# Nine raw weight buffers in the room of a smaller DMA scratch

## The chip, the cores and the metric

The kernel runs on one core of a Trainium2 chip. The core has a matrix engine (PE, with its weight loads told apart as PEld), a vector engine (DVE), a scalar engine (ACT), a general engine (POOL) and a queue engine that only issues and waits (SP). Each runs its own instructions in order. DMA transfers are issued by SP, ACT or POOL and run beside the engines. The metric is the time of one execution on the device in microseconds; lower is better.

## The reference

One layer (DEPTH is 1) of a streaming encoder with 256 frames of 2048 channels, all in float32. Cut to what matters:

```python
mod = silu(c) @ w_ada + b_ada                    # 6 vectors of 2048
sh1, sc1, g1, sh2, sc2, g2 = split(mod, 6)
h = rmsnorm(x, norm_g[0]) * (1 + sc1) + sh1
y = token_mixer(h, ...)                          # h @ w_in (2048 x 10256), linear attention with a
                                                 # forget gate, a gated short convolution, merge, @ w_o
x = x + g1 * rmsnorm(y, norm_g[1])
h = rmsnorm(x, norm_g[2]) * (1 + sc2) + sh2
gate, up = split(h @ w_up, 2)                    # 2048 x 11264
y = (gelu(causal_dwconv(gate)) * up) @ w_down    # 5632 x 2048
x = x + g2 * rmsnorm(y, norm_g[3])
```

`c` is a single vector, so `silu(c) @ w_ada` is a product of a vector with a matrix of 2048 x 12288. The weights are read once each.

## The kernel before

**Tiles and chunks.** All weights pass through the core as a *stream* of pieces, in the order in which they are used. A piece is loaded into a raw buffer, prepared, and used. There are three kinds:

- `Chunk`: 256 rows by 512 columns of a weight (128 partitions x 1024 floats, 512 KB). `dma` loads it (L278). `split` writes a rounded copy on ACT (`whi`, L283) and the rest on DVE (`wlo = raw - whi`, L292). `mm` multiplies it on PE, as three products: high by high, high by low and low by high. Groups of the kind `Feat` (L346) keep the weight still, groups of the kind `Tok` (L401) the activations.
- `Gemv`: 128 rows by 1024 columns of `w_ada` (512 KB, L431). It has no matmul: DVE adds `raw * silu(c)[k]` to a running sum (L439).
- `Ada`: the same for the first two vectors, which `h` needs (loads at L465, updates at L479), by slices of the channels.

When a sum of gemvs is complete, `fold` (L204 to L212) transposes it into a raw buffer (L209) and reduces it (L211).

**Raw buffers.** All of these take their buffer from one pool of `RAW_BUFS` tiles of 4 KB of a partition, under the tag `raw`. A buffer comes free when its last reader is done, which for a chunk is the split on DVE.

**What sets the order.** `pump` (L510) goes through the stream. For each piece it first issues loads ahead, then splits ahead, then multiplies:

```python
while pos[0] < min(len(stream), i + 1 + look_dma) and pos[0] < pos[1] + RAW_BUFS:
    stream[pos[0]].dma()
    pos[0] += 1
while pos[1] < min(len(stream), i + 1 + LOOK_SPLIT, ...):
    ...
```

`pos[0]`, `pos[1]` and `pos[2]` count the pieces loaded, split and multiplied. Splits run up to four pieces ahead of the matmuls (`LOOK_SPLIT`), loads up to ten (`LOOK_DMA`), which is also four and the six raw buffers. The framework's planner then lays out each engine's queue by its own costs, the priorities and the buffers that it takes to be free; it may place an instruction earlier than the text has it.

**The stages.** First come the pieces of `Ada` for the first slice of channels, the norm of `x` and the start of `h`. Then the input projection runs in five slices of the channels, with the gemvs merged in between the chunks (L918 to L933). It is followed by the rest of the token mixer, `late` (L935 to L959): the output of the convolution, the gates, the linear attention's heads beside them as small steps (`gla_heads`, L746: per head two groups of small matmuls, L758 and L772, a square on ACT, L776, a sum on DVE, L779, and a matmul with ones, L782), its output and `w_o`. `to_rows` (L816) sends the vectors g1 and g2 through DRAM and back to all partitions, with DMAs that POOL issues (L824, L827); these rows are read at L841 and L1027. Between the halves stands a norm (from L1128, with `x` loaded again at L1116). Then the channel mixer runs in three parts of `w_up` and `w_down`.

[...]

Of the kernel before, what the change touches and what calls it, by code (L numbers as in the profile page):

```python
# [34 lines left out]
C_CB, C_CC, C_CX = 3088, 4112, 5136  # L35
C_GA, C_GB = 6160, 8208

RAW_BUFS, SPLIT_BUFS, LOOK_SPLIT, LOOK_DMA = 6, 4, 4, 10
T1 = 4
T2 = 4  # L40
G8 = 4
# [1180 lines left out]
```

## Time and profile before

| | us |
|---|---|
| median of 3 runs | 1451.01 |
| lowest, highest | 1450.29, 1453.19 |
| the profiled execution | 1448.84 |
| its span, from first to last instruction | 1447.1 |
| mean granted clock of PE | 0.993 |

The profile tells of one execution. A row of a group has the line, the engine, the operation, the tiles written and read, how many there were, the time they were busy, the mean of one in ns, and the idle time of the engine before them with what ended it. A row of the timeline has the start, the time it took, the engine, the line, the operation and its tiles; in brackets stands how long the engine was idle before it and who ended that. A row of the waits has who waited for whom, the sum in us, how often, and the longest. `SPq` is SP's queue, which issues the loads. Matmuls overlap, so the busy time of PE counts a matmul until its modelled end. An idle engine costs something only where the end of the kernel waits for it.

### The profile page before, as it was taken

The numbers are of one execution on the slowest core, as the hardware profiler recorded it, in microseconds if no ns is written. First come the engines' busy times: TensorE is split into PE (matmuls) and PEld (weight loads), VectorE is DVE, ScalarE is ACT, GpSimd is POOL, SyncE is SP. The second block draws the span as 40 slices with busy tenths as digits, with TensorE's granted clock in tenths as the row PEclk, the third lists the DMA queues.
The fourth block names the chain that finished last, engine by engine and source line by source line (L and its number), as shares of the span: only waits on it lengthen the run. The fifth ranks groups of instructions, "written<-read, shape, count | busy, mean of one in ns | idle before, by whom it ended". The sixth has DMA issues, their size and how long they took to land.

```text
span 1447.1 us, 23205 instructions
## 1 busy us (share of the span) xinstructions
PE 1407.4 (97%) x9107; PEld 1262.5 (87%) x9107; DVE 1058.6 (73%) x1194; ACT 816.9 (56%) x995; POOL 6.1 (0%) x40
## 2 busy tenths in 40 slices
PE   6999999999999998999999999999999999999997
PEld 6898999898999998988898888888888888888886
DVE  6878888888888777976798777556767645566565
ACT  5789776688574554444665554444545533445553
POOL 0000000000000000000000000000000000000000
PEclk9999999999999999999999999999999999999999
DMA  9999999998979777897467777777786656666652
GB/s 318 329 329 329 373 317 334 335 307 293 355 249 327 244 257 269 293 313 246 134 201 243 227 243 231 248 236 233 230 251 202 217 195 190 186 196 190 190 185 95
DMA packets 177896, 366.82 MB, mean 253 GB/s; under 512 B 13803, under 2 KB 26457, under 8 KB 177018
## 3 DMA queue, kind: packets, MB, share of 16 engines
q1 hardware_dynamic: 176857, 362.17, 76.0%
q0 software_dynamic: 352, 2.11, 0.4%
q8 instruction: 71, 1.16, 0.3%
q10 hardware_dynamic: 576, 1.05, 0.2%
q14 instruction: 40, 0.32, 0.1%
HBM read 363.18 MB, written 2.11 MB: 252 GB/s over the span
## 4 chain that ended last, share of the span: by engine, by line
PE 76%; DMA 11%; DVE 7%; ACT 3%; issue 2%; SPq 0%; DVEq 0%; ACTq 0%
PE mm L346 50%; PE mm L401 25%; DMA raw<-in_w_ada_dram 7%; DMA raw<-in_w_in_dram 4%; DVE wlo L292 2%; ACT whi L283 1%; DVE c L439 1%; DVE c L479 1%; DVE fold L211 0%; PE sm L1152 0%; ACT mm L323 0%; DVE raw L209 0%; PE sm L782 0%; ACT t L257 0%; DVE XF L1138 0%
## 5 line engine op out<-in xcount | busy, mean ns | idle before, releaser
L283 ACT CAST whi<-raw 128x1024 fp32r<-128x1024 f32 (+1 forms) x503 | 513.1, 1025 | 499.1 <-PE mm L346 202.9
L292 DVE TENSOR_TENSOR wlo<-raw,whi 128x1024 fp32r<-128x1024 f32 (+1 forms) x503 | 594.7, 1190 | 245.9 <-ACT whi L283 242.0
L346 PE MATMUL mm<-H,whi 128*128 128x256 f32 (+2 forms) x3712 | 656.9, 321 | 2.2 <-ACT H L254 1.2
L346 PEld LDWEIGHTS mm<-H,whi 128*128 128x128 f32 x3712 | 527.8, 189 | 51.5 <-ACT whi L283 1.7
L346 PE MATMUL mm<-H,wlo 128*128 128x256 f32 (+1 forms) x2496 | 365.9, 278 | 1.4 <-DVE wlo L292 1.4
L346 PEld LDWEIGHTS mm<-H,wlo 128*128 128x128 f32 x2496 | 332.6, 188 | 14.4 <-DVE wlo L292 1.6
L401 PE MATMUL mm<-whi,g 128*128 128x512 f32 x704 | 178.3, 391 | 0.0
L401 PEld LDWEIGHTS mm<-whi,g 128*128 128x128 f32 x704 | 131.9, 188 | 29.1
L439 DVE SCALAR_TENSOR_TENSOR c<-raw,sil,c 128x1024 f32<-128x1024 f32 x90 | 115.3, 1281 | 42.3 <-DMA raw<-in_w_ada_dram 42.1
L401 PE MATMUL mm<-whi,H 128*128 128x512 f32 x448 | 117.5, 394 | 4.2 <-ACT whi L283 4.2
L401 PEld LDWEIGHTS mm<-whi,H 128*128 128x128 f32 x448 | 82.9, 188 | 24.0 <-ACT whi L283 6.4
L401 PE MATMUL mm<-wlo,g 128*128 128x512 f32 x352 | 98.1, 392 | 0.0
L479 DVE SCALAR_TENSOR_TENSOR c<-raw,sil,c 128x768 f32<-128x768 f32 (+2 forms) x73 | 78.6, 1077 | 8.8 <-DMA raw<-in_w_ada_dram 8.1
L401 PEld LDWEIGHTS mm<-wlo,g 128*128 128x128 f32 x352 | 66.1, 188 | 14.1
L401 PE MATMUL mm<-wlo,H 128*128 128x512 f32 x224 | 65.3, 393 | 0.0
L439 DVE SCALAR_TENSOR_TENSOR cb<-raw,sil,cb 128x1024 f32<-128x1024 f32 x30 | 38.5, 1284 | 24.8 <-DMA raw<-in_w_ada_dram 24.8
L401 PEld LDWEIGHTS mm<-wlo,H 128*128 128x128 f32 x224 | 42.2, 188 | 9.0
L618 DVE SCALAR_TENSOR_TENSOR t<-pt,fcol,t 128x256 f32<-128x256 f32 x88 | 36.6, 481 | 0.0
L346 PE MATMUL mm<-B,whi 128*128 128x256 f32 x256 | 33.4, 283 | 0.0
L346 PEld LDWEIGHTS mm<-B,whi 128*128 128x128 f32 x256 | 30.8, 188 | 2.6 <-issue 1.2
L346 PE MATMUL mm<-g,whi 128*128 128x256 f32 x256 | 32.3, 279 | 0.0
L346 PEld LDWEIGHTS mm<-g,whi 128*128 128x128 f32 x256 | 30.8, 190 | 0.0
(196 smaller groups left out, 740.8 us busy)
## 6 DMA issues: line engine op xcount, KB each, us to landing
raw<-in_w_up_dram SPq DMA_DIRECT2D x176, 512.0 KB, 4.3
raw<-in_w_ada_dram SPq DMA_DIRECT2D x160, 512.0 KB, 5.5
raw<-in_w_in_dram SPq DMA_DIRECT2D x145, 512.0 KB, 5.5
raw<-in_w_down_dram SPq DMA_DIRECT2D x88, 512.0 KB, 4.3
raw<-in_w_o_dram SPq DMA_DIRECT2D x32, 512.0 KB, 5.5
raw<-in_w_ada_dram SPq DMA_DIRECT2D x32, 384.0 KB, 5.6
raw<-in_w_out_conv_dram SPq DMA_DIRECT2D x16, 512.0 KB, 5.3
raw<-in_w_out_gla_dram SPq DMA_DIRECT2D x16, 512.0 KB, 5.0
```

Source lines behind the costliest of these rows:

```text
L283: nc.scalar.copy(self.hi, self.raw)
L292: nc.vector.tensor_sub(self.lo, self.raw, f(self.hi))
L346: nc.tensor.matmul(out, w[:, t, j * P:(j + 1) * P], x, start=first_in_bank and t == 0 and i == 0, stop=end and t == ch.n - 1 and i == 2, s ...
L401: nc.tensor.matmul(self.out[s], m(c.k0 + t, T)[:, s * P:(s + 1) * P], w[:, t, :], start=first and t == 0 and i == 0, stop=end and t == c.n ...
L439: nc.vector.scalar_tensor_tensor(a, self.raw, sil[:, self.k:self.k + 1], a, op0=ALU.mult, op1=ALU.add)
L479: nc.vector.scalar_tensor_tensor(a, raw, sc, a, op0=ALU.mult, op1=ALU.add)
L618: nc.vector.scalar_tensor_tensor(dst[:, a, :], pt[:, a, i:T + i], w(i, a), dst[:, a, :], op0=ALU.mult, op1=ALU.add)
```

## The change

The scratch for dynamic DMAs is set to 4 KB of a partition. The raw pool has nine buffers instead of six, and loads are issued up to thirteen pieces ahead of the matmuls instead of ten. The other look-aheads and all instructions of the text stay as they are.

```diff
-RAW_BUFS, SPLIT_BUFS, LOOK_SPLIT, LOOK_DMA = 6, 4, 4, 10
+RAW_BUFS, SPLIT_BUFS, LOOK_SPLIT, LOOK_DMA = 9, 4, 4, 13
...
-    nc = _bacc.Bacc("TRN2", target_bir_lowering=False, num_devices=1)
+    nc = _bacc.Bacc("TRN2", target_bir_lowering=False, num_devices=1, dynamic_dma_scratch_size=4096)
```

## The prediction

> **What bounds the kernel now.** I read the page first (busy shares, the 40 slices, the chain by line, the landing times), then the windows view stage by stage, then the waits of PE and of SP.
>
> ```profile
> PE 1407.4 (97%) x9107; PEld 1262.5 (87%) x9107; DVE 1058.6 (73%) x1194; ACT 816.9 (56%) x995; POOL 6.1 (0%) x40
> DMA  9999999998979777897467777777786656666652
> PE 76%; DMA 11%; DVE 7%; ACT 3%; issue 2%; SPq 0%; DVEq 0%; ACTq 0%
> raw<-in_w_in_dram SPq DMA_DIRECT2D x145, 512.0 KB, 5.5
> ```
>
> The stages, from the windows view:
>
> ```profile
> 0.00:40.00 40.00, 27.15 (x199) 26.08 (x200) 25.90 (x43) 23.89 (x37) 1.39 (x12) 0.96 0.96 320
> 40.00:600.00 560.00, 544.06 (x4406) 519.38 (x4405) 465.62 (x495) 379.44 (x432) 1.59 (x6) 0.99 0.91 310
> 600.00:680.00 80.00, 80.00 (x382) 66.86 (x382) 61.60 (x57) 37.01 (x46) 0.00 (x0) 1.00 0.85 286
> 680.00:720.00 40.00, 36.89 (x226) 32.54 (x225) 27.59 (x49) 24.85 (x50) 0.00 (x0) 0.91 0.47 141
> 720.00:1440.00 720.00, 719.29 (x3902) 617.61 (x3900) 474.29 (x547) 351.36 (x430) 3.10 (x22) 1.00 0.66 209
> ```
>
> The columns of a window are: PE, PEld, DVE, ACT and POOL busy, the granted clock, the DMA share, GB/s. There are two regimes. From 720 us on PE is idle for 0.71 of 720 us while DMA runs at 0.66: earlier loads have nothing to end there. From 600 to 680 PE is never idle. From 680 to 720 PE loses 3.1 us in the norm between the halves, which waits for no weight. So what the change can win lies before 600, and what is won there reaches the end, because PE is full from there on but for that norm. Between 40 and 600 PE is idle for 560 - 544.06 = 15.9 us, DVE is busy for 83% and DMA for 91%. The chain's 11% of DMA (some 160 us) is therefore not what the loads cost: nearly all of it runs beside PE. The price is PE's idle time, and the waits of PE in that stretch split it:
>
> ```profile
> PE sm L782 <- DVE t L779: 6.3, 2, 5.9
> PE mm L401 <- ACT whi L283: 4.2, 5, 1.2
> PE sm L1093 <- DVE gg L872: 1.9, 1, 1.9
> PE mm L346 <- DVE wlo L292: 1.4, 1, 1.4
> PE sm L782 <- DVE s L870: 1.2, 1, 1.2
> ```
>
> They sum to 15.0 us, and two groups under 0.5 us are left out: that, and what they cost in clock, is the ceiling of this change after the first 40 us.
>
> **The change part by part.** *Three more raw buffers.* [...] No instruction is added: the same loads are issued, earlier. How far earlier follows from the loads between 40 and 600, as the DMA view of that stretch groups them (packets, MB, share of 16 engines):
>
> ```profile
> q1 hardware_dynamic: 81314, 171.64, 89.7%
> ```
>
> 171.64 MB are 327 loads of 512 KB (0.524 MB) in 560 us, one each 1.71 us. A buffer of six comes round every 10.3 us, of which 5.5 are the load; nine come round every 15.4 us. So a load may be up to 5.1 us earlier, which is more than the waits for a load below. SP's own waits show that buffers not yet read, by the split on DVE above all, hold the loads back:
>
> ```profile
> SPq L278 <- DVE wlo L292: 582.4, 333, 11.4
> ```
>
> Now the terms, each by the stall it takes away.
>
> (a) *562 us, the last head of the linear attention.* PE stands in front of the ones-matmul of L782, which needs L779 on DVE; L779 stands in DVE's queue behind a gemv update (L439) that waits for its load.
>
> ```profile
> 549.89 1.29 DVE L439 SCALAR_TENSOR_TENSOR c<-raw,sil,c 128x1024 f32<-128x1024 f32 x1 [0.85 <-DMA raw<-in_w_ada_dram]
> 554.90 2.36 DVE L292 TENSOR_TENSOR wlo<-raw,whi 128x1024 fp32r<-128x1024 f32 x2
> 560.91 1.28 DVE L439 SCALAR_TENSOR_TENSOR c<-raw,sil,c 128x1024 f32<-128x1024 f32 x1 [3.65 <-DMA raw<-in_w_ada_dram]
> 562.11 0.42 DVE L779 TENSOR_TENSOR t<-t 128x256 f32<-128x256 f32 x1
> 562.58 1.22 PE L782 MATMUL sm<-t,ones 128*128 128x256 f32 x2 [5.88 <-DVE t L779]
> ```
>
> Up to 5.1 us earlier covers the 3.65. At least 3.65 of 5.88 us go if only this wait goes; all of it if the update before (DVE waited 0.85 us for its load at 549.89) lets DVE reach L779 sooner still. I take the middle, 4.8.
>
> (b) *The granted clock behind that stall.*
>
> ```profile
> 560.00:564.00 4.00, 1.42 (x4) 1.24 (x5) 2.13 (x3) 0.16 (x1) 0.00 (x0) 0.50 0.63 231
> 564.00:568.00 4.00, 4.00 (x30) 3.99 (x29) 3.26 (x5) 1.71 (x3) 0.23 (x1) 0.80 0.70 236
> ```
>
> Busy time at a lower clock costs 1.42 x 0.50 + 4.00 x 0.20 = 1.5 us. With a stall of 0 to 2 us most of that goes: 1.2. If a shorter stall drops the clock as well, nothing goes.
>
> (c) *The five waits of L401 for whi, 4.2 us.* In each ACT's cast had just waited for its load, as in the first:
>
> ```profile
> 52.59 1.04 ACT L283 CAST whi<-raw 128x1024 fp32r<-128x1024 f32 x1 [1.34 <-DMA raw<-in_w_in_dram]
> 53.69 2.11 PE L401 MATMUL mm<-whi,H 128*128 128x512 f32 x8 [1.21 <-ACT whi L283]
> 57.53 2.11 PE L401 MATMUL mm<-whi,H 128*128 128x512 f32 x8 [0.81 <-ACT whi L283]
> ```
>
> SP's issues before that, in order of time:
>
> ```profile
> 18.13 0.37 SPq L278 DMA_DIRECT2D raw<-in_w_in_dram  x1
> 22.64 0.37 SPq L465 DMA_DIRECT2D raw<-in_w_ada_dram  x1
> ```
>
> The two before 60 us cost 2.0. SP issues nothing between 18.5 and 22.6 us for want of a buffer; three loads put there fill that hole and arrive before the waits, so I take 2.0. The other three (2.2 us together, between 270 and 290 us) lie where DMA is nearly full, so a lead must have been saved up earlier: I take half, 1.1.
>
> (d) *355 us.*
>
> ```profile
> 352.63 1.05 ACT L283 CAST whi<-raw 128x1024 fp32r<-128x1024 f32 x1 [1.53 <-DMA raw<-in_w_in_dram]
> 355.07 0.28 PE L1093 MATMUL sm<-ident,t 66*128 66x66 f32 x1 [1.88 <-DVE gg L872]
> ```
>
> PE waits 1.9 us at L1093 for DVE, whose split waited for ACT, whose cast had waited 1.53 us for a load. Not all of that is slack, since ACT also runs long there: 1.0. The 1.4 us of L346 for wlo come from that rush on ACT and DVE, not from a load: 0.
>
> (e) *508 us.*
>
> ```profile
> 506.57 1.28 DVE L439 SCALAR_TENSOR_TENSOR c<-raw,sil,c 128x1024 f32<-128x1024 f32 x1 [1.40 <-DMA raw<-in_w_ada_dram]
> ```
>
> PE waits 1.2 us there for L870. DVE had waited 1.40 us for a load in front of L779 and L870: 1.2.
>
> The sum: 4.8 + 1.2 + 3.1 + 1.0 + 1.2 = 11.3 us. At most, with all of those waits but the 1.4 (13.6), the two small groups and 1.5 of clock, it is near 16; the first 40 us may add some 2, since the loads that start them are at a DMA share of 0.96 already, so the end is near 18.
>
> *The smaller scratch.* [...]
>
> ```profile
> q0 software_dynamic: 352, 2.11, 0.4%
> 570.06 0.56 POOL L827 DMA_DIRECT2D g<-row_g  x1 [1.67 <-DMA row_g<-t]
> L841 DVE TENSOR_TENSOR A<-mm,g x3: 1217/1220/1225, 633.6 to 674.2; 128x1024 f32<-128x1024 f32 x3
> ```
>
> The row is asked for at 570 and first read at 633.6 us. The matmuls of those 63 us hide it, so I cost it at nothing; if it landed later than that, each us would count. [...]
>
> *What else moves.* The x loads of L1116 and the small loads of the gates stand in SP's queue behind three more weight loads, some 5.1 us.
>
> ```profile
> 570.01 1.01 SPq L1116 DMA_DIRECT2D XF<-in_x_dram  x2
> ```
>
> x serves the norm after 680 us, so that is covered by over 100 us of matmuls.
>
> **From the profile to the median.** The profiled execution took 1448.84 us (span 1447.1), 2.2 us under the median of 1451.01. Its sum is 1448.84 - 11.3 = 1437.5; against the median 1451.0 - 11.3 = 1439.7, which I forecast.
>
> **The rivals.** *(1) DMA is full up to 400 us.* Its digits there are nines. Then a lead can't be saved up, (c) gives nothing and the rest, 8.2 us, stays: 1442.8. Against it, single stretches run faster than the mean of 310 GB/s:
>
> ```profile
> 140.00:160.00 20.00, 20.00 (x179) 20.00 (x178) 17.63 (x16) 16.79 (x18) 0.00 (x0) 1.00 1.03 379
> 572.00:576.00 4.00, 4.00 (x38) 4.00 (x37) 2.52 (x4) 2.11 (x2) 0.00 (x0) 1.00 1.03 414
> ```
>
> [...]
>
> *(2) The gain is given back.* DVE is busy 465.6 of 560 us and in order; with loads in time the next late thing may be DVE's queue or ACT's casts, and PE's waits keep their length with another name. That would show as the same 15 us of idle PE without waits for DMA: 1449 to 1452, forecast 1451. A build that pays no heed to the scratch belongs here as well.
>
> *(3) Slower: the planner's order on DVE.* The order on each queue isn't that of the text: the load of L1087 stands behind all the slices in the code, yet SP issues it at 24.45 us, and its reader, L1093, runs near 355 us.
>
> ```profile
> 24.45 0.42 SPq L1087 DMA_DIRECT2D t<-in_ffn_conv_w_dram  x1
> ```
>
> With the loads forecast earlier the planner may put gemv updates ahead of the steps of the heads. Each costs 1.28 us in front of L779, for which PE stands still. (a), (b) and (e), 7.2 us, would be lost, and 4.1 would be left of the sum. One more update ahead of each of four heads costs 5.1 us: from there on it is slower. Three more cost 15.4, so 1451 + 15.4 - 4.1 = 1462. Against it: the updates would be drawn from the same number, and would be missing later, where DVE also has room.
>
> **How the numbers follow.** Forecast (8 to 18 us gained) 0.60; rival 1 0.15; rival 2 0.15; rival 3 0.10. Within 0.2% is 2.9 us, about what a measurement of this kernel tells from no change. So faster 0.75, same 0.15, slower 0.10. The range goes from 1451 - 18 and 3 us for the spread of the runs, 1430, to the upper end of rival 2, 1452; rival 3 and the tails lie outside.
>
> **What would show it.**
>
> ```profile
> ACT whi L283 <- DMA raw<-in_w_in_dram: 60.4, 50, 4.3
> ```
>
> Right: DVE's wait for the load at 560.91 and PE's 5.88 us at L782 are gone or under 2.2 us, the clock stays at 1.00 from 560 to 568, the five waits of L401 shrink to under 2 us together, these 60.4 us of ACT's waits for w_in halve, landing times rise above 5.5 us because more loads are in flight, and PE's idle time from 40 to 600 is near 6 us. After 720 us nothing changes. Wrong: DMA waits gone but PE's idle time as before (rival 2); another order on DVE with longer waits at L782 (rival 3); waits of L401 as before at a DMA share of 0.97 (rival 1). [...]

## The result, and the profile after

The kernel with nine buffers takes 1439.59 us (median of 5 runs, 1437.15 to 1445.49), the one before beside it 1451.87 us (1450.29 to 1457.29). The ratio is 0.9924, with a 95% interval of 0.9905 to 0.9944: 0.8% faster. The profiled execution took 1438.51 us (span 1436.6).

The page of the kernel after has these lines that answer to those of before: busy time by engine, DMA's busy tenths and its rate in 40 slices, the chain by engine, and the landing time of the loads of `w_in`.

```profile
PE 1403.6 (98%) x9107; PEld 1262.7 (88%) x9107; DVE 1055.3 (73%) x1194; ACT 817.5 (57%) x995; POOL 6.1 (0%) x40
DMA  9999989989979788986467767777776666666651
GB/s 334 380 355 318 390 288 376 337 292 344 369 246 321 244 256 286 300 299 196 132 205 255 239 226 238 250 237 227 237 247 191 218 192 192 190 192 190 189 178 59
PE 88%; DMA 5%; DVE 4%; issue 1%; ACT 1%; SPq 0%; DVEq 0%; ACTq 0%
raw<-in_w_in_dram SPq DMA_DIRECT2D x145, 512.0 KB, 6.1
```

The chain has 5% of DMA instead of 11%, and loads land later after their issue (6.1 instead of 5.5 us), as was forecast for more loads in flight at once. The windows of the same stages:

```profile
0.00:40.00 40.00, 26.43 (x184) 25.56 (x185) 25.10 (x42) 23.09 (x36) 1.39 (x12) 0.91 0.99 339
40.00:600.00 560.00, 551.32 (x4496) 529.97 (x4496) 477.65 (x511) 387.50 (x441) 1.59 (x6) 0.99 0.92 319
680.00:720.00 40.00, 37.00 (x262) 34.61 (x262) 31.03 (x59) 26.31 (x54) 0.00 (x0) 0.91 0.47 142
```

PE's idle time from 40 to 600 fell from 15.9 to 8.7 us. What is left is in the waits of PE from 30 to 600 us:

```profile
PE sm L782 <- DVE t L779: 4.5, 1, 4.5
PE sm L782 <- DVE s L870: 2.2, 1, 2.2
PE sm L1093 <- DVE gg L872: 0.8, 1, 0.8
PE sm L758 <- DVE t L790: 0.7, 1, 0.7
PE sm L217 <- DVE fold L211: 0.2, 1, 0.2
```

The waits for the splits, of L401 for `whi` (4.2 us before) and of L346 for `wlo` (1.4), are gone. The waits of the heads at L782 are still there: 6.7 us instead of 7.5. So the time came out as forecast, but not with the amounts that the forecast had for each place.

To see the places, cut at 400 us. Before, then after:

```profile
40.00:400.00 360.00, 351.56 (x2765) 333.49 (x2764) 300.27 (x314) 272.99 (x316) 0.41 (x4) 1.00 0.96 330
400.00:600.00 200.00, 192.50 (x1643) 185.89 (x1643) 165.35 (x182) 106.44 (x117) 1.18 (x2) 0.98 0.82 272
```

```profile
40.00:400.00 360.00, 358.77 (x2874) 343.44 (x2874) 310.63 (x328) 280.47 (x323) 0.41 (x4) 1.00 0.97 343
400.00:600.00 200.00, 192.55 (x1623) 186.53 (x1623) 167.02 (x184) 107.03 (x119) 1.18 (x2) 0.98 0.83 275
```

From 40 to 400 us PE's idle time falls from 8.4 to 1.2 us; from 400 to 600 it is 7.5 us in both. A mark that both kernels pass says what this is worth. L713 is the first matmul behind the input projection that occurs only there (a row of the line's view: shortest, median and longest in ns, first and last start in us). Before, then after:

```profile
L713 PE MATMUL sm<-t,t x4: 589/641/693, 408.0 to 412.5; 33*128 33x512 f32 x4
```

```profile
L713 PE MATMUL sm<-t,t x4: 589/641/693, 395.8 to 400.3; 33*128 33x512 f32 x4
```

PE is there 12.2 us earlier, and the span is 10.5 us shorter: in these two executions the whole gain is made before the mark, and some 1.7 us are given back behind it. Idle time is only a part of the 12.2 us. Here are the windows from the start to the mark, before, after, and in `nine_again`, another execution of the kernel after, which passes the mark at 400.9 us:

```profile
0.00:408.00 408.00, 386.71 (x3029) 367.34 (x3029) 333.72 (x364) 300.46 (x355) 1.80 (x16) 1.00 0.95 328
0.00:395.80 395.80, 381.00 (x3030) 365.68 (x3030) 331.82 (x365) 300.29 (x355) 1.80 (x16) 0.99 0.98 344
0.00:400.90 400.90, 386.63 (x3029) 370.51 (x3029) 332.41 (x365) 299.65 (x355) 1.80 (x16) 1.00 0.96 340
```

Idle time falls from 21.3 to 14.8 us, and in `nine_again` to 14.3: this part, 6.5 to 7.0 us, repeats. The other 5.7 us are busy time for the same number of matmuls, 386.7 against 381.0 us, and `nine_again` doesn't have them. Where PE runs only the matmuls of L346, in the kernel after and then in `nine_again`:

```profile
220.00:260.00 40.00, 40.00 (x355) 40.00 (x355) 34.22 (x32) 28.22 (x29) 0.00 (x0) 1.00 1.05 389
220.00:260.00 40.00, 40.00 (x342) 40.00 (x341) 34.30 (x31) 27.17 (x29) 0.00 (x0) 1.00 1.03 375
```

PE is never idle and has the full clock in both, yet one begins 355 matmuls and the other 342 in the same 40 us, one each 112.7 and 117.0 ns. So one program can run 4% slower for a stretch with no wait that the profile shows. What causes this is open. Over the traces of this document, PE's idle time up to the mark is 20.2 to 24.2 us where six buffers were used up to there (four traces) and 13.6 to 15.4 us with nine (seven traces, two of them of the kernel after); the busy time is 384.5 to 387.6 and 381.0 to 386.7 us. The idle time is what the buffers are shown to save; that they act on the busy time too is likely, but not shown.

### The profile page after: what moved, and what is told of

It reads as the page before. It is cut to its first block, busy times and chain, and to the rows that moved or that the text cites. A ratio compares the mean times of both kernels' runs of the same rounds, so it can differ in the third digit from the quotient of the medians.

```text
span 1436.6 us, 23116 instructions
## 1 busy us (share of the span) xinstructions
PE 1403.6 (98%) x9107; PEld 1262.7 (88%) x9107; DVE 1055.3 (73%) x1194; ACT 817.5 (57%) x995; POOL 6.1 (0%) x40
## 4 chain that ended last, share of the span: by engine, by line
PE 88%; DMA 5%; DVE 4%; issue 1%; ACT 1%; SPq 0%; DVEq 0%; ACTq 0%
PE mm L346 60%; PE mm L401 27%; DMA raw<-in_w_ada_dram 3%; DVE wlo L292 2%; DMA raw<-in_w_in_dram 1%; DVE c L439 1%; DVE c L479 1%; DMA XF<-in_x_dram 1%; ACT whi L283 0%; PE sm L1152 0%; DVE fold L211 0%; SPq L465 0%; DVE raw L209 0%; PE sm L782 0%; PE sm L758 0%
## 5 line engine op out<-in xcount | busy, mean ns | idle before, releaser
L346 PE MATMUL mm<-H,whi 128*128 128x256 f32 (+2 forms) x3712 | 656.0, 321 | 1.3 <-ACT H L254 1.2
L346 PEld LDWEIGHTS mm<-H,whi 128*128 128x128 f32 x3712 | 528.1, 190 | 49.3 <-ACT H L254 1.3
L346 PE MATMUL mm<-H,wlo 128*128 128x256 f32 (+1 forms) x2496 | 365.3, 278 | 0.0
L346 PEld LDWEIGHTS mm<-H,wlo 128*128 128x128 f32 x2496 | 332.1, 188 | 12.8
L401 PE MATMUL mm<-whi,g 128*128 128x512 f32 x704 | 178.2, 391 | 0.0
L401 PEld LDWEIGHTS mm<-whi,g 128*128 128x128 f32 x704 | 131.9, 188 | 29.2
L439 DVE SCALAR_TENSOR_TENSOR c<-raw,sil,c 128x1024 f32<-128x1024 f32 x90 | 115.0, 1278 | 33.7 <-DMA raw<-in_w_ada_dram 33.6
L401 PE MATMUL mm<-whi,H 128*128 128x512 f32 x448 | 116.3, 392 | 0.0
L401 PEld LDWEIGHTS mm<-whi,H 128*128 128x128 f32 x448 | 83.4, 188 | 17.9
L401 PE MATMUL mm<-wlo,g 128*128 128x512 f32 x352 | 98.1, 392 | 0.0
L401 PEld LDWEIGHTS mm<-wlo,g 128*128 128x128 f32 x352 | 66.1, 188 | 14.1
L401 PE MATMUL mm<-wlo,H 128*128 128x512 f32 x224 | 65.1, 393 | 0.0
L439 DVE SCALAR_TENSOR_TENSOR cb<-raw,sil,cb 128x1024 f32<-128x1024 f32 x30 | 38.5, 1282 | 33.9 <-DMA raw<-in_w_ada_dram 33.7
L401 PEld LDWEIGHTS mm<-wlo,H 128*128 128x128 f32 x224 | 42.1, 188 | 8.9
L346 PE MATMUL mm<-g,whi 128*128 128x256 f32 x256 | 33.7, 285 | 0.0
L346 PE MATMUL mm<-B,whi 128*128 128x256 f32 x256 | 33.4, 283 | 0.0
L346 PEld LDWEIGHTS mm<-B,whi 128*128 128x128 f32 x256 | 30.8, 188 | 2.6 <-ACT whi L283 2.0
L346 PEld LDWEIGHTS mm<-g,whi 128*128 128x128 f32 x256 | 31.9, 193 | 0.1
## 6 DMA issues: line engine op xcount, KB each, us to landing
raw<-in_w_up_dram SPq DMA_DIRECT2D x176, 512.0 KB, 3.9
raw<-in_w_ada_dram SPq DMA_DIRECT2D x160, 512.0 KB, 5.5
raw<-in_w_in_dram SPq DMA_DIRECT2D x145, 512.0 KB, 6.1
raw<-in_w_down_dram SPq DMA_DIRECT2D x88, 512.0 KB, 4.3
raw<-in_w_o_dram SPq DMA_DIRECT2D x32, 512.0 KB, 5.6
raw<-in_w_out_conv_dram SPq DMA_DIRECT2D x16, 512.0 KB, 7.0
raw<-in_w_out_gla_dram SPq DMA_DIRECT2D x16, 512.0 KB, 5.0
```

The lines of the kernel that those rows point to most:

```text
L346: nc.tensor.matmul(out, w[:, t, j * P:(j + 1) * P], x, start=first_in_bank and t == 0 and i == 0, stop=end and t == ch.n - 1 and i == 2, s ...
L401: nc.tensor.matmul(self.out[s], m(c.k0 + t, T)[:, s * P:(s + 1) * P], w[:, t, :], start=first and t == 0 and i == 0, stop=end and t == c.n ...
L439: nc.vector.scalar_tensor_tensor(a, self.raw, sil[:, self.k:self.k + 1], a, op0=ALU.mult, op1=ALU.add)
```

## The experiments

The line numbers of a kernel with added lines are higher by those lines. The kernel before ran beside each group; over 25 runs it took 1444.6 to 1458.5 us, so single times say little, and the ratios below come with their intervals.

### Which half of the change, and how far ahead the text may load

`scratch_only` has the small scratch and six buffers:

```diff
-RAW_BUFS, SPLIT_BUFS, LOOK_SPLIT, LOOK_DMA = 9, 4, 4, 13
+RAW_BUFS, SPLIT_BUFS, LOOK_SPLIT, LOOK_DMA = 6, 4, 4, 10
```

> Scratch of 4 KB, but six raw buffers and loads ten pieces ahead as before. If the buffers give the whole gain, this takes the time of before, 1451 within 3 us, with the same idle time of PE between 40 and 600 us (15.9 us). If the smaller scratch itself had a part in it (POOL's row loads, another place of the buffers in memory), it would be faster or slower by that part.

Measured: 1450.63 us, ratio 1.0003 (0.9978 to 1.0028), with 13.5 us of idle PE from 40 to 600 us. The scratch makes no difference to the time that can be measured. Whether nine buffers would fit beside the scratch of before, no run shows.

`nine_look10` has nine buffers and the look-ahead of before:

```diff
-RAW_BUFS, SPLIT_BUFS, LOOK_SPLIT, LOOK_DMA = 9, 4, 4, 13
+RAW_BUFS, SPLIT_BUFS, LOOK_SPLIT, LOOK_DMA = 9, 4, 4, 10
```

> Nine raw buffers, but the text issues loads only ten pieces ahead. Theory: the planner issues a load as soon as a buffer is free, wherever the text has it, so the buffers alone count: 1440 within 3 us. Rival: the look-ahead of the text bounds the loads, four pieces of splits and six of loads as before: 1451 within 3 us.

Measured: 1435.0 us, ratio 0.9891 (0.9867 to 0.9915). That is 2 us below the range of the theory and far from the rival: the buffers alone give the gain, and the look-ahead of the text doesn't bound the loads. The traces show it too, if the loads of the chunks, as SP issues them, are paired in order with ACT's casts. From 40 to 400 us the median *lead*, the time from the issue of a load to its first use, is 6.4 us before, 10.7 us after and 10.5 us in `nine_look10`. `nine_again`, the kernel after itself beside the next group:

> The kernel after itself, on the chip of the next three: 0.992 of the kernel before, within 0.3%.

Measured: 1441.63 us, ratio 0.9931 (0.9901 to 0.9961). `nine_look10` differs from it in a small part of the order on the queues. The intervals overlap, so that it is the faster of the two is likely, but not shown.

### Where the gain is made

`early_nine` has nine buffers up to the end of the input projection and six behind it, `late_nine` the other way round. They take buffers in turn from a pool of six and one of three, and use the second only on their side of the boundary:

```diff
+    def raw_tile(shape):
+        nine = pos[0] <= stream.index(early_to)
+        turn[0] += 1
+        if nine and turn[0] % 3 == 2:
+            own[0] = ("rawb", RAW_B)
+        else:
+            own[0] = ("raw", RAW_A)
+        return sb(shape, *own[0])
...
-            while pos[0] < min(len(stream), i + 1 + look_dma) and pos[0] < pos[1] + RAW_BUFS:
+            while pos[0] < min(len(stream), i + 1 + look_dma) and pos[0] < pos[1] + room():
```

> Nine buffers (six and three, taken in turn) up to the last chunk of the input projection, only six of them after it. Theory: the gain is made in the input projection, before about 400 us, where ACT's casts waited for their loads, and none of it in the stretch of the heads: 1440 within 3 us, with the stall of PE at L782 near 550 us as long as in the kernel after (4.5 us). Rival, the prediction's split of the sum: some 7 of 11 us come from 400 to 600 us, so 1447.

> Six buffers up to the last chunk of the input projection, nine after it. Theory: no gain, 1451 within 3 us. Rival, the prediction's split: 7 us of gain, 1444.

Measured: 1446.6 us, ratio 0.9977 (0.9963 to 0.9991), and 1457.35 us, ratio 1.0041 (1.0024 to 1.0059). Neither theory nor rival gave both times: `early_nine` takes what the rival said, but by the rival `late_nine` would have won 7 us, and it lost some. The mark behind the input projection (L713, here L732, its weight load) and the windows of the heads say why. The line's view of `early_nine`, then of `late_nine`:

```profile
L732 PEld LDWEIGHTS sm<-t,t x4: 183/184/186, 397.0 to 401.1; 33*128 33x128 f32 x4
```

```profile
L732 PEld LDWEIGHTS sm<-t,t x4: 183/184/186, 411.8 to 415.9; 33*128 33x128 f32 x4
```

And the window of the heads, in the same order:

```profile
400.00:600.00 200.00, 188.49 (x1577) 182.62 (x1577) 155.07 (x171) 103.01 (x116) 1.18 (x2) 0.97 0.79 262
```

```profile
400.00:600.00 200.00, 190.61 (x1560) 183.02 (x1559) 156.64 (x171) 104.01 (x114) 1.18 (x2) 0.96 0.79 264
```

Nine buffers before the boundary bring PE to the mark at 397.0, 11 us earlier than before: the gain of the input projection is there. Behind the mark some 7.5 of them are lost again, 4 as idle time in the heads, where PE is idle for 11.5 us instead of 7.5. With six buffers first the mark comes at 411.8, 4 us later than before, and nine buffers in the heads leave 9.4 us of idle time there: they don't help. Two pools also change the planner's order, so the price of the order and that of the buffers can't be told apart in these two; that needed the next group.

### Why the heads kept their stalls

At 550 us in the kernel after, by SP, DVE and PE of its timeline:

```profile
544.25 0.34 SPq L431 DMA_DIRECT2D raw<-in_w_ada_dram  x1
544.14 2.35 DVE L292 TENSOR_TENSOR wlo<-raw,whi 128x1024 fp32r<-128x1024 f32 x2
549.61 0.75 DVE L436 TENSOR_SCALAR c<-raw,sil 128x1024 f32<-128x1024 f32 x1 [3.12 <-DMA raw<-in_w_ada_dram]
550.28 0.42 DVE L779 TENSOR_TENSOR t<-t 128x256 f32<-128x256 f32 x1
550.75 0.48 PE L782 MATMUL sm<-t,ones 128*128 128x256 f32 x1 [4.54 <-DVE t L779]
```

It is the picture of before. DVE stands 3.12 us for the load of a gemv update, issued 5.4 us ago, and L779 and PE stand behind it. Nine buffers didn't bring this load forward. The waits by line, before and after, show the two kinds of load apart:

```profile
DVE c L439 <- DMA raw<-in_w_ada_dram: 42.1, 35, 3.6
DVE cb L439 <- DMA raw<-in_w_ada_dram: 24.8, 16, 3.1
```

```profile
DVE cb L439 <- DMA raw<-in_w_ada_dram: 33.7, 22, 3.3
DVE c L439 <- DMA raw<-in_w_ada_dram: 33.6, 22, 4.1
ACT whi L283 <- DMA raw<-in_w_in_dram: 16.3, 14, 3.9
```

ACT's waits for chunks of `w_in` fall from 60.4 to 16.3 us, DVE's for gemv updates stay (66.9 and 67.3 us). The leads show them apart as well, with the loads of gemvs paired in order with their updates. In the heads, from 400 to 600 us, the median lead of a chunk rises from 8.5 to 18.0 us, that of a gemv update only from 5.7 to 5.8. (From 40 to 400 us both rise, from 6.4 to 10.7 and from 6.8 to 9.9.) The explanation to be tested: a chunk that has landed waits for a split buffer, so a deeper pool puts it further ahead; a gemv update needs no split buffer, and the planner puts it in DVE's queue where by its own costs the load has landed. If the load comes later than that, everything behind it on DVE stands. The test is to take that freedom away: an update may not stand ahead of the split of the chunk that is before it in the stream. `issue_after` only orders the queue.

```diff
-                nc.vector.tensor_sub(self.lo, self.raw, f(self.hi))
+                last_lo[:] = [nc.vector.tensor_sub(self.lo, self.raw, f(self.hi)).ins]
...
         def split(self):
+            with tc.issue_after(last_lo[0]):
+                self.update()
+
+        def update(self):
             if self.k == 0:
```

> The kernel after, with each gemv update held on DVE's queue behind the split of the chunk that stands before it in the stream (an order on the queue, no wait of its own). Theory: with nine buffers the chunks' loads are 10 to 22 us ahead of their casts, but a gemv update still runs 5 us after its load was issued, because the planner puts it where its load lands by the planner's costs; DVE then stands for the load with a head's step (L779) behind it. In order, the loads are issued as far ahead as the chunks', DVE's waits for w_ada loads fall from 67 us to under 30, the stalls of PE at L782 from 6.7 to under 3 us, and the time by 4 to 7 us to about 1434. Rival: DVE has too much work there in any order; the stalls stay and the time is that of the kernel after, 1440.

> The same order with six buffers and the scratch as before. Theory: six buffers leave no lead (4 us beyond a landing), so the casts keep waiting for loads, and holding an update back keeps its buffer longer: no gain in the input projection, 1446 to 1454. Rival: the order alone is worth it, 1444, and the number of buffers doesn't matter for it.

Measured: `nine_in_order` 1428.06 us, ratio 0.9847 (0.9826 to 0.9868); `six_in_order` 1442.64 us, ratio 0.9948 (0.9933 to 0.9964). In `nine_in_order` DVE's waits of gemv updates for their loads and PE's waits at L782 are gone from the lists of waits (forecast: under 30 and under 3 us left), so its rival is refuted. The order is worth more than was expected, and it is worth 9 us with six buffers too: there the rival was right. With six buffers it takes PE's idle time in the heads from 7.5 to 2.5 us and leaves that up to the mark nearly as it was, 20.2 us. Each half alone gives about the same, nine buffers 10 to 12 us and the order 9, and both together 23: they act in different places.

To place the order, `order_late` holds the updates back only behind the input projection (`if pos[1] > stream.index(early_to)` ahead of the `issue_after`), and `order_early` only up to it.

> Nine buffers; gemv updates are held in order on DVE only behind the last chunk of the input projection. Theory: what the order won (some 12 us beside the kernel after) is won in the stretch of the heads, where a head's step stood behind an update that waited for its load: 1430 within 3 us, 0.986 of the kernel before. Rival: the order helps by keeping the input projection's buffers in step: 1438 to 1442.

> Nine buffers; gemv updates are held in order only up to the last chunk of the input projection. Theory: the heads keep their stalls, 1440 within 3 us, with stalls of PE at L782 of 4 us or more. Rival: 1430.

Measured: `order_late` 1428.82 us, ratio 0.9839 (0.9807 to 0.9871); `order_early` 1434.57 us, ratio 0.9881 (0.9850 to 0.9913), with one stall of 5.2 us left at L782. The order behind the input projection gives all that `nine_in_order` has. `order_early` is some 5 us faster than expected, as `nine_look10` was, and its interval overlaps with those of `nine_again` and `order_late`, so the times don't exclude that the order up to there has a share. Three kernels with nine buffers and stalls in the heads (`nine_look10`, `order_early` and the kernel after) lie between 1434.6 and 1441.6 us, with 4.3, 5.9 and 7.5 us of idle PE from 400 to 600 us; why they differ is open. The windows of `order_late`:

```profile
40.00:400.00 360.00, 357.63 (x2843) 342.24 (x2842) 307.76 (x324) 277.85 (x321) 0.41 (x4) 1.00 0.96 340
400.00:600.00 200.00, 199.96 (x1679) 192.72 (x1679) 173.63 (x191) 113.04 (x124) 1.18 (x2) 1.00 0.83 283
```

From 400 to 600 PE is idle for 0.04 us instead of 7.45, and the clock is granted in full. The median lead of a gemv update is 15.9 us there instead of 5.8. At the place of the stall (L439 is L447 here, L779 is L787) the update no longer waits; its load was issued at 524.99 us:

```profile
541.67 1.28 DVE L447 SCALAR_TENSOR_TENSOR c<-raw,sil,c 128x1024 f32<-128x1024 f32 x1
542.87 0.42 DVE L787 TENSOR_TENSOR t<-t 128x256 f32<-128x256 f32 x1
```

DVE does as many gemv updates from 400 to 600 us as in the kernel after, 38, so it wasn't short of time; it stood in the wrong place.

### How many buffers

> Seven buffers, loads eleven pieces ahead. A load can be 1.7 us earlier. The waits of PE for casts in the input projection were 0.3 to 1.2 us each, those of the rush near 339 and 355 us 1.4 and 1.9. Theory (many short waits): already more than half of the gain, 1443 to 1446. Rival: the gain grows evenly with the buffers, a third, 1447.

Measured: 1454.55 us, ratio 1.0027 (1.0011 to 1.0043): slower than before, which neither the theory nor the rival had. It passes the mark early, and loses the time behind it. Its line's view of L713, its waits of PE from 720 us on, and its timeline at the first of these:

```profile
L713 PE MATMUL sm<-t,t x4: 589/641/693, 397.7 to 402.2; 33*128 33x512 f32 x4
```

```profile
PE mm L346 <- DVE t L975: 4.3, 4, 1.3
PE mm L346 <- DVE pt L975: 3.1, 5, 0.8
```

```profile
790.83 1.28 DVE L439 SCALAR_TENSOR_TENSOR cb<-raw,sil,cb 128x1024 f32<-128x1024 f32 x1 [2.03 <-DMA raw<-in_w_ada_dram]
792.77 1.20 PE L346 MATMUL mm<-H,whi 128*128 128x512 f32 x4 [1.31 <-DVE t L975]
```

At the mark it is 10.3 us ahead of the kernel before, at the end of the span 4.7 us behind: 15.0 us are lost in between. Half of them are named here. The updates of the last modulation vector, in the channel mixer, stand for their loads in front of the step that empties PE's accumulators (L975), 9 times; this costs 7.4 us of PE in a stage where the kernel before loses nothing. It is the fault of the heads in another place, and without it, by an estimate from these numbers, the kernel would be 2.7 us ahead. The same number of buffers with the order set, and eight (seven: `RAW_BUFS` 7, `LOOK_DMA` 11; eight: 8 and 12):

> All gemv updates in order, seven buffers. With the order fixed, the number of buffers acts on the input projection alone. The kernel with seven buffers lost 17 us of PE's time there against 29 before and 14 with nine. Theory: 1451.5 - 9 (order) - 11 = 1431 within 3 us. Rival: the kernel with seven buffers was slower than before because seven are too few: 1440 or more.

> All gemv updates in order, eight buffers. Theory: between seven and nine, 1428 to 1432; the last buffer brings 2 us or less. Rival: each buffer brings the same, 1433.

Measured: 1437.18 us, ratio 0.9891 (0.9851 to 0.9932), between the theory and the rival, and 1431.46 us, ratio 0.9857 (0.9824 to 0.9889), as the theory had it. (The first expectation's 29 us of lost time before aren't borne out by the windows up to the mark: PE is idle for 21.3 us before, for 16.2 with seven buffers and 14.8 with nine.) With the order set, six, seven, eight and nine buffers give 1442.6, 1437.2, 1431.5 and 1428.1 us. The intervals of seven and eight overlap, and so do those of eight and nine, so what each buffer adds isn't shown. That seven have most of the gain isn't borne out with the order set: PE's idle time up to the mark is 20.2, 19.5, 14.3 and 14.6 us, in one execution each. Why seven do worse with the order than without, 19.5 against 16.2 us, is open. The leads of the chunks hardly tell: from 40 to 400 us their median is 7.2 us with the order and 7.5 without.

## Why the prediction was right, and where it wasn't

The forecast, 1439.7, and the median, 1439.59, agree, but that they agree so closely is luck. The forecast put 7.2 of its 11.3 us into the heads, which gave nothing. The input projection gave some 7 us of idle time instead of 4.1, and the rest of the measured 12.3 us (9.9 in the group of `nine_again`) isn't tied to a wait by any trace.

**(c) and (d), the input projection: right mechanism, too small.** The forecast had 3.1 + 1.0 = 4.1 us. From 40 to 400 us PE's idle time fell by 7.2 us (6.9 in `nine_again`), and the waits account for it. All five waits of L401 went (4.2 us), those inside the full stretch too, so the half that was held back for them in (c) wasn't needed. The wait at L1093 fell from 1.9 to 0.8 us, as (d) had it. The 1.4 us of L346 for `wlo`, costed at nothing as a rush on ACT and DVE, went as well, and so did 0.4 us of L346 for `whi`. Beyond this, PE's busy time up to the mark was 5.7 us less in one execution of the kernel after and 0.1 us less in the other; the forecast had no term for it. The first 40 us, which were to add some 2 us at most, gave nothing: PE is idle for 13.6 us there instead of 12.9.

**(a), (b), (e), the heads: wrong.** The forecast had 7.2 us, and the runs showed none: PE's idle time from 400 to 600 us is 7.5 us before and after. The step that failed is "a load may be up to 5.1 us earlier", read for all loads from the mean turn of a buffer. In the heads it holds for chunks, whose lead grew by 9.5 us, and not for gemv updates, whose lead grew by 0.1. The stall of 5.88 us is one of 4.54, that in front of L870 is 2.2 instead of 1.2, and the clock drops behind both. In the kernel after:

```profile
548.00:552.00 4.00, 1.25 (x7) 1.20 (x8) 1.09 (x2) 1.43 (x3) 0.00 (x0) 0.94 0.88 327
552.00:556.00 4.00, 4.00 (x25) 3.99 (x25) 3.00 (x3) 1.02 (x1) 0.00 (x0) 0.64 0.61 219
```

And around the stall in front of L870:

```profile
493.50:496.90 3.40, 1.48 (x13) 1.28 (x11) 1.44 (x2) 2.33 (x2) 0.00 (x0) 1.00 0.91 301
496.90:500.30 3.40, 3.09 (x12) 2.91 (x13) 2.06 (x5) 0.47 (x1) 0.00 (x0) 0.50 0.70 216
```

In the trace before, waits of PE of 1.88 and 1.2 us, inside the 0 to 2 us of (b), had 1.00 of the clock behind them (355.0 to 358.4 and 508.6 to 512.0 us). In the kernel after, 0.64 is granted behind the stall of 4.54 us, from 552 to 556. `order_late`, which has no stall from 400 to 600 us, has 1.00 there. At the stall of 2.23 us in front of L870, PE was busy for 1.48 of the 3.40 us up to 496.9, and 0.50 was granted for the next 3.4. So a stall of less than half the 5.88 us dropped the clock as well, the case in which (b) said that nothing goes.

**The scratch** costs nothing that can be measured, as forecast: 1.0003. Which DMAs it serves was not shown. In the kernel after, the row g is asked for at 558.8 us and first read at 620.3, so it still has over 60 us.

**The rivals.** *Rival 1*, DMA full up to 400 us, is refuted: from 40 to 400 us DMA moved 343 GB/s instead of 330, and (c) came in full. *Rival 2*, the gain given back to other waits, holds for the heads, though the wait there has kept its name and isn't DVE's work. *Rival 3*, the planner's order on DVE, was given 0.10 for this kernel and didn't come about in it. Yet what it looked at, where the planner puts the gemv updates on DVE, decides the heads, and the kernel with seven buffers is slower than before without the order and faster with it.

**The signs.** Right: the waits of L401, ACT's waits for `w_in`, the landing times, nothing changed after 720 us. Wrong: L782 and the clock. PE's idle time from 40 to 600 was forecast near 6 us and is 8.7.

## What to carry to other kernels

In the heads the deeper pool put only the loads of chunks further ahead: from 400 to 600 us their median lead grew by 9.5 us, that of gemv updates by 0.1. What a planner puts where it expects the load to land can stay late, as it did there with nine buffers as with six, and then the order on the engine that stands for the load (DVE here, 3.12 us at 549.61) is the thing to change. Where a planner orders the queues, look for instructions that wait for a load with a short step of another chain behind them, and pin the former behind work that is due earlier. Here that pin, set behind the input projection alone, doubled the gain of the buffers: 0.9839 instead of 0.9924. And compare two executions of one kernel before a difference of two traces is put down to the change: here the place of a mark differed by 5.1 us between them.

## What the runs showed of the hardware that was not expected

Matmuls of one form ran at two paces under the same full clock and without idle time, one each 112.7 and 117.0 ns over 40 us, in two executions of one kernel; the cause is open. A stall of PE of 2.23 us was followed by half the clock for 3.4 us. And DMA moved 390 GB/s over a slice of 36 us (373 in the same slice before), where the mean from 40 to 600 us before was 310.
